# Steps of 512 instead of 256 columns for q, k, v, z and the output projection of a two-layer mixer and mixture-of-experts kernel

## The chip, the cores and the metric

The kernel is one program on one core of a Trainium2 chip. Its time is the device time in microseconds of one execution. The engines are named as in the profile: PE multiplies matrices (PEld is its weight load), DVE and ACT work element by element, POOL is the fourth compute engine, SP issues most of the DMAs. Each engine works through its own queue in order, so an instruction that waits holds up everything behind it on that engine.

## The reference

Two layers over 512 tokens (256 context tokens and 256 latent tokens) of width 1024. The first half of a layer is a mixer of three branches:

```python
h = modulate(x, c)                                    # (512 tokens, 1024)
q, k, v, lru_x, lru_gate, z, xbc, dt, gates = split(h @ w_in)
att = diff_attn(rope(q), rope(k), v)                  # 4 heads, 2 maps each
lru = rglru_bidir(conv(lru_x)) * gelu(lru_gate)       # two linear scans over time
ssd = norm(mamba2_bidir(conv(xbc), dt) * silu(z))     # chunks of 128 tokens
m   = sum(sigmoid(gate_br) * (branch_br @ w_branch[br]) for br in 3)
x   = LN(alpha * x + gate * (m @ w_out))
```

The second half is a mixture of 64 experts (8 per token) and a shared one, with which the change has nothing to do. q, k, v and z are 512 columns each of `w_in`; `w_out` is 1024 by 1024. The second layer needs q, z and the output only for the 256 latent tokens.

## The kernel before

All products that the change touches are made of three matmuls per 128 rows of the sum: activations and weights are split into a high and a low part, and high*high, high*low and low*high are added up in one PSUM bank (`tok`, L566; `w_out`, L1094). The sum has 1024 rows, so a product takes 8 x 3 = 24 matmuls. The activations of a block of 128 tokens are the stationary operand, the weights move through: 256 columns at a time.

The weights come from HBM in chunks of 1 MB (`Main`, L505): 1024 rows of 256 columns. `load` brings a chunk into one of two buffers, `split` makes the high part on ACT and the low part on DVE (two instructions each), `next(i)` splits chunk i+1 and hands out chunk i. `order` says which chunks come when: four of xbc, two of lx, then q, k, v for the first 256 columns and q, k, v for the second, two of lg (the gate of the LRU), two gates g(1,0) and g(1,1), two of z, and the other ten gates. The four chunks of `w_out` follow.

For q and k, each block of 128 tokens goes through one loop step: `tok` puts 24 matmuls into one of the two "mm" banks; `flush(1)` issues the PE transposes of an earlier block's result; three DVE multiplies and a POOL add apply the rotary embedding (blocks 0 and 1) or an ACT copy takes the block out of PSUM (blocks 2 and 3); `side.pump(2.6)` issues a few pieces of side work. v has an ACT copy in place of the rotary embedding. Transposed halves land in the two "tr" banks, from which a DVE copy takes them.

The side work is a set of Python generators (class `Side`, L175): the steps of the SSD branch, of the LRU, of attention and of the modulation for the next layer. `pump` picks the first one whose last step is done by a small clock model, and issues its next step on all engines at once, behind what stands in their queues. `need` issues all that is left of some generators. It is called ahead of lg (all of the LRU), and ahead of g(1,0) (all of the SSD and the LRU).

After the mixer, `w_out` runs over the four (second layer: two) blocks of 128 tokens, a pair of 256-column calls for each 512-column bank, all in the "mm" banks.

Of the kernel before, what the change touches and what calls it, by code (L numbers as in the profile page):

```python
# [13 lines left out]
AF = mybir.ActivationFunctionType  # L14
# [4 lines left out]
P = 128  # L19
# [211 lines left out]
def tile_kernel(ctx: ExitStack, tc: tile.TileContext, A: dict, out: bass.AP):  # L231
# [306 lines left out]
    def feat(hT, w, j, t0, t1, p):  # L538
# [4 lines left out]
            PE.matmul(p[:, t0:t1], w[1][:, k, c], hT(0, k)[:, t0:t1], start=False, stop=k == KD - 1)  # L543
        return p

    def mixer(l, main, order, hT, pre, late):
        last = l == DEPTH - 1
        prm = LP[l]
# [14 lines left out]
        def xt(n):  # L563
            return xA[:, n, :] if n < 4 else xB[:, n - 4, :]

        def tok(w, b, n=256):  # L566
            p = bank("mm")
            c = slice(b * P, (b + 1) * P)
            for k in range(KD):
                PE.matmul(p[:, :n], hT(0, k)[:, c], w[0][:, k, :n], start=k == 0, stop=False)  # L570
                PE.matmul(p[:, :n], hT(0, k)[:, c], w[1][:, k, :n], start=False, stop=False)
                PE.matmul(p[:, :n], hT(1, k)[:, c], w[0][:, k, :n], start=False, stop=k == KD - 1)
            return p
# [281 lines left out]
        def flush(keep=0):  # L855
            while len(pend) > keep:
                dst, r = pend.pop(0)
                pt = bank("tr")
                for h in range(2):
                    PE.transpose(pt[:, h * P:(h + 1) * P], r[:, h * P:(h + 1) * P], ident)  # L860
                V.tensor_copy(dst, pt[:, :256].rearrange("p (h t) -> p h t", h=2))
# [7 lines left out]
                G.tensor_tensor(x_, x_, sg, op=OP.mult)  # L869

        for i, (kind, arg) in enumerate(order):
            w = main.next(i)
            if kind == "lx":
                for j in range(2):
                    n = 2 * arg + j
# [38 lines left out]
                    silu()  # L914
                    g_ssd = side.add(ssd())
            elif kind in "qk":
                if late and kind == "k" and arg == 0:
                    side.add(late)
                dst = (qT if kind == "q" else kT)[:, 2 * arg:2 * arg + 2, :]
                for b in range(nb if kind == "q" else 4):  # L920
                    p = tok(w, b)[:, :256]
                    flush(1)
                    r = tmp()
                    if b < 2:
                        pv = p.rearrange("p (g a f) -> p g a f", g=4, a=2)
                        rv = r[:, :256].rearrange("p (g a f) -> p g a f", g=4, a=2)
                        tv = r[:, 256:].rearrange("p (g a f) -> p g a f", g=4, a=2)
                        V.tensor_mul(rv, pv, rope[:, b, None, None, 0:32].to_broadcast([P, 4, 2, 32]))
                        V.tensor_mul(tv[:, :, 0, :], pv[:, :, 1, :], nsin[:, b, None, :].to_broadcast([P, 4, 32]))
                        V.tensor_mul(tv[:, :, 1, :], pv[:, :, 0, :], rope[:, b, None, 32:64].to_broadcast([P, 4, 32]))  # L930
                        G.tensor_tensor(r[:, :256], r[:, :256], r[:, 256:], op=OP.add)
                    else:
                        S.activation(r[:, :256], p, AF.Copy)
                    pend.append((dst[:, :, b * P:(b + 1) * P], r))
                    side.pump(2.6)
            elif kind == "v":
                for b in range(4):
                    p = tok(w, b)
                    S.activation(vt[:, b, arg * 256:(arg + 1) * 256], p[:, :256], AF.Copy)
                    flush()  # L940
                    side.pump(2.6)
                units += [(2 * arg + h, b) for b in range(nb) for h in range(2)]
                if arg == 1:
                    state["qkv"] = 1
            elif kind == "lg":
                side.need(g_lru)
                if arg == 1 and g_ssd not in side.q:
# [8 lines left out]
                    side.pump(nw)  # L956
            elif kind == "z":
                side.need(g_ssd)
                for b in range(nb):
                    p = tok(w, b)[:, :256]  # L960
                    c = slice(arg * 256, (arg + 1) * 256)
                    z = tmp()
                    S.activation(z[:, :256], p, AF.Sigmoid)
                    V.tensor_mul(z[:, :256], z[:, :256], p)
                    G.tensor_tensor(yd[:, b, c], yd[:, b, c], z[:, :256], op=OP.mult)
                    if arg == 1:
                        LN.setdefault("norm", []).append(side.add(ssd_norm(b)))
                    side.pump(2.6)
            else:
                br, jq = arg  # L970
                ib = 4 * (1, 2, 0).index(br) + jq
# [84 lines left out]
    def sublayer2(l, mg, wo, R):  # L1056
# [36 lines left out]

        def w_out(b, q):  # L1094
            if q % 2 == 0:
                hvs.setdefault(b, []).append(bank("mm"))
            p = hvs[b][-1]
            tk = slice(b * P, (b + 1) * P)
            c = slice(q % 2 * 256, (q % 2 + 1) * 256)
            w = wo[len(order) + q]  # L1100
            for k in range(KD):
                PE.matmul(p[:, c], mg(0, k)[:, tk], w[0][:, k, :], start=k == 0, stop=False)
                PE.matmul(p[:, c], mg(0, k)[:, tk], w[1][:, k, :], start=False, stop=False)
                PE.matmul(p[:, c], mg(1, k)[:, tk], w[0][:, k, :], start=False, stop=k == KD - 1)

        def norm1(b):
            x_ = xr(b)
# [773 lines left out]
    cols += [("w_out", q) for q in range(4)]  # L1881


    mains = [Main(l, cols) for l in range(DEPTH)]
# [178 lines left out]
def _tiles(a, rows, cols):  # L2063

    *lead, r, c = a.shape
    a = a.reshape(*lead, r // (rows * P), rows, P, c // cols, cols)
    n = len(lead)
    a = a.transpose(*range(n), n, n + 3, n + 2, n + 1, n + 4)
    return a.reshape(*lead, r // (rows * P) * (c // cols), P, rows * cols)


def _layouts(inputs):
    import numpy as np
    a = {n: np.asarray(inputs[n]) for n in _INS}
    w = a["w_in"]
    a["w_in"] = np.concatenate([_tiles(w[:, :, :C_DT], KD, 256), _tiles(w[:, :, C_G:], KD, 256)], axis=1)
    a["w_dt"] = _tiles(w[:, :, C_DT:C_G], KD, 16)[:, 0]
    for n in ("w_mod", "w_out"):
        a[n] = _tiles(a[n], KD, 256)
# [31 lines left out]
```

## Time and profile before

| | us |
|---|---|
| median of 3 runs | 2388.75 |
| lowest and highest | 2381.78 and 2395.73 |
| the profiled execution, its own time | 2394.08 |
| its span | 2392.3 |
| PE busy in the span | 2197.0 (92%) |
| mean granted TensorE clock | 0.963 |

In a timeline row the first number is the start in the span, the second the time from the first instruction's start to the last one's end; xN is how many instructions the row holds, and the bracket how long the engine had stood idle before the row and whose result ended that. In a table of windows each engine has its busy time and its count of instructions, followed by the granted TensorE clock (1.00 is 2.4 GHz, 0.50 is 1.2 GHz). The stretches that the change touches: in layer 0, q, k and v from 133.9 to 263.85 us, lg and the forced end of SSD and LRU from 263.85 to 304.25, z from 363.5 to 407, the output projection from 608.3; in layer 1, 1519.2 to 1616.3, 1616.3 to 1640, 1645 to 1670, and from 1788.9.

### The profile page before, as it was taken

Reading aid. Unit: us, or ns where it says so; the run is one execution under the profiler, and the core shown is the slowest. Engines: PE = TensorE matmul, PEld = TensorE weight load, DVE = VectorE, ACT = ScalarE, POOL = GpSimd, SP = SyncE. Lnnn points to the kernel's source line nnn. Section 1 sums busy time; section 2 is a strip of 40 time slices with the busy share of each in tenths; the row PEclk is TensorE's granted clock in tenths of the full one; section 3 lists DMA queues with packets and bytes.
Section 4 is the critical chain, followed back from the end, with each engine's and each line's share of the span. In section 5 each row is a group of like instructions: output and inputs, shape, how many; then the busy total and the mean of one; then the engine's idle time right before and its main releaser. Section 6 shows DMA issues by size and latency. Waiting matters only on the chain. (4 is left out here: it accounts for less than half of the span.)

```text
span 2392.3 us, 37529 instructions
## 1 busy us (share of the span) xinstructions
PE 2197.0 (92%) x14847; PEld 1383.5 (58%) x14847; DVE 1038.9 (43%) x2325; ACT 701.4 (29%) x1270; POOL 450.2 (19%) x388
## 2 busy tenths in 40 slices
PE   7999999999979999999998849998999899999997
PEld 5778767777954334333333228787996444554553
DVE  3756355433653323332222166656665323333333
ACT  3465356423221111111111124655652111111111
POOL 0223111021113223233232144441110000000000
PEclk8999989999979999999999969998999999999999
DMA  7333333453658999999999942113447689999992
GB/s 296 145 139 109 126 125 112 161 186 133 229 224 288 358 375 350 358 354 351 343 354 353 377 147 76 69 70 102 141 169 304 263 360 421 379 420 420 421 420 92
DMA packets 107219, 605.24 MB, mean 253 GB/s; under 512 B 18216, under 2 KB 18560, under 8 KB 42784
## 3 DMA queue, kind: packets, MB, share of 16 engines
q1 hardware_dynamic: 91608, 560.97, 60.6%
q0 software_dynamic: 13952, 41.57, 7.2%
q8 instruction: 118, 1.93, 0.3%
q10 hardware_dynamic: 1480, 0.27, 0.1%
q14 instruction: 61, 0.50, 0.1%
HBM read 576.54 MB, written 31.06 MB: 254 GB/s over the span
## 5 line engine op out<-in xcount | busy, mean ns | idle before, releaser
L149 PE MATMUL mm<-s,t 128*32 128x512 f32 (+3 forms) x4320 | 664.1, 565 | 29.1 <-DMA s<-in_w_up_dram 26.6
L149 PE MATMUL mm<-s,s 128*128 128x256 f32 (+1 forms) x3488 | 561.8, 319 | 13.5 <-DVE tm L149 8.1
L149 PEld LDWEIGHTS mm<-s,s 128*128 128x128 f32 x3488 | 491.1, 194 | 70.3 <-issue 17.9
L149 PEld LDWEIGHTS mm<-s,t 128*32 128x32 f32 (+2 forms) x4320 | 262.8, 127 | 363.4 <-issue 300.3
L149 DVE TENSOR_TENSOR tm<-tm,mm 128x256 f32<-128x256 f32 (+3 forms) x194 | 85.7, 442 | 559.4 <-ACT tm L149 506.8
L149 ACT ACTIVATE tm<-mm 128x256 f32<-128x256 f32 (+3 forms) x155 | 65.1, 421 | 729.3 <-PE mm L149 720.1
L149 DVE TENSOR_TENSOR s<-s,s 128x1024 fp32r<-128x1024 f32 (+4 forms) x170 | 202.3, 1231 | 46.3 <-ACT s L149 43.8
L149 PE MATMUL sd<-s,tm 128*32 128x512 f32 (+2 forms) x1112 | 182.3, 626 | 21.5 <-DMA s<-in_w_down_dram 21.1
L149 POOL DMA_INDIRECT acc<-s,si x77 | 111.1, 1442 | 461.9 <-ACT t L149 226.8
L149 PE MATMUL sd<-s,s 128*128 128x512 f32 (+4 forms) x768 | 183.5, 454 | 12.2 <-ACT t L149 11.2
L149 PEld LDWEIGHTS sd<-s,s 128*128 128x128 f32 (+2 forms) x768 | 112.1, 188 | 68.4 <-issue 33.3
L149 ACT ACTIVATE s<-s 128x1024 fp32r<-128x1024 f32 (+3 forms) x168 | 148.4, 937 | 7.4 <-PE sd L149 6.1
L149 PEld LDWEIGHTS tr<-t,s 128*128 128x128 f32 x1024 | 123.8, 196 | 44.3 <-issue 41.5
L149 PEld LDWEIGHTS sd<-s,tm 128*32 128x32 f32 (+2 forms) x1112 | 54.7, 122 | 142.4 <-issue 114.8
L149 PE MATMUL tr<-t,s 128*128 128x128 f32 (+1 forms) x1024 | 132.6, 284 | 1.4 <-ACT s L149 1.0
L149 POOL TENSOR_TENSOR s<-s,tm 128x512 f32<-128x512 f32 (+1 forms) x52 | 64.0, 1232 | 318.6 <-ACT tm L149 157.3
L149 PE MATMUL mm<-s,tm 128*32 128x512 f32 (+1 forms) x760 | 109.0, 599 | 13.9 <-ACT tm L149 10.2
L149 ACT ACTIVATE t<-tr 128x512 f32<-128x512 f32 (+6 forms) x115 | 62.1, 544 | 184.2 <-PE tr L149 171.6
L149 POOL TENSOR_TENSOR t<-t,mhalf 128x2 f32<-128x2 f32 x1 | 0.7, 702 | 562.9 <-DVE t L149 562.9
L149 PEld LDWEIGHTS tr<-ident,s 128*128 128x128 f32 (+2 forms) x568 | 67.7, 150 | 65.4 <-issue 44.7
L149 PE MATMUL tr<-ident,s 128*128 128x128 f32 (+2 forms) x568 | 83.3, 292 | 24.1 <-DVE s L149 18.4
L149 ACT ACT_TABLE_LOAD x63 | 80.8, 1283 | 39.0 <-PE mm L149 12.9
(255 smaller groups left out, 2161.6 us busy)
## 6 DMA issues: line engine op xcount, KB each, us to landing
s<-in_w_up_dram SPq DMA_DIRECT2D x256, 1024.0 KB
s<-in_w_down_dram SPq DMA_DIRECT2D x128, 1024.0 KB
s<-in_w_in_dram SPq DMA_DIRECT2D x56, 1024.0 KB
s<-in_w_mod_dram SPq DMA_DIRECT2D x48, 1024.0 KB
t<-in_w_branch_dram SPq DMA_DIRECT2D x32, 256.0 KB
s<-in_w_out_dram SPq DMA_DIRECT2D x8, 1024.0 KB
acc<-t SPq DMA_DIRECT2D x4, 1280.0 KB
s<-in_ws_up_dram SPq DMA_DIRECT2D x4, 1024.0 KB
```

Source lines behind the costliest of these rows:

```text
L149: r = f(*a, **k)
```

## The change

The weights of q, k, v, z and `w_out` are laid out in other chunks of 1 MB: 512 rows of 512 columns ("half 0" and "half 1" of the rows). A product of 1024 rows and 512 columns needs two chunks; its 24 matmuls are 512 wide, and it fills a whole bank. The number of chunks, of buffers and of bytes stays.

`tok` takes the blocks of tokens in pairs: 12 matmuls of half 0 for the first block and 12 for the second, then 12 of half 1 for each. Only then are the two results handed on, one after the other, with the same steps as before for each of their 256-column halves. So four steps of flush, rotary embedding and pump follow one another, where before one step followed each 24 matmuls. v and z have one 512-wide step per block. The order of chunks is q, q, k, k, v, v. In `w_out` the banks alternate between "mm" and "sd".

```diff
-        def tok(w, b, n=256):
-            p = bank("mm")
-            c = slice(b * P, (b + 1) * P)
-            for k in range(KD):
-                PE.matmul(p[:, :n], hT(0, k)[:, c], w[0][:, k, :n], start=k == 0, stop=False)
...
+        def tok(i, blocks):
+            main.split(i + 1)
+            hl = [wide(main.hl.pop(i + q)) for q in range(2)]
+            for b0 in range(0, blocks, 2):
+                bs = range(b0, min(b0 + 2, blocks))
+                ps_ = {b: bank("mm") for b in bs}
+                for q in range(2):
+                    if q and b0 + 2 >= blocks:
+                        main.split(i + 2)
+                    for b in bs:
+                        p, c, w = ps_[b], slice(b * P, (b + 1) * P), hl[q]
+                        for k in range(4):
+                            kk = 4 * q + k
+                            PE.matmul(p, hT(0, kk)[:, c], w[0][:, k, :], start=kk == 0, stop=False)
+                            PE.matmul(p, hT(0, kk)[:, c], w[1][:, k, :], start=False, stop=False)
+                            PE.matmul(p, hT(1, kk)[:, c], w[0][:, k, :], start=False, stop=kk == KD - 1)
+                for b in bs:
+                    yield b, ps_[b]
...
-                for b in range(nb if kind == "q" else 4):
-                    p = tok(w, b)[:, :256]
-                    flush(1)
...
+                for b, pp in tok(i, nb if kind == "q" else 4):
+                    for hh in range(2):
+                        p = pp[:, hh * 256:(hh + 1) * 256]
+                        flush(1)
...
-                    S.activation(vt[:, b, arg * 256:(arg + 1) * 256], p[:, :256], AF.Copy)
+                for b, p in tok(i, 4):
+                    S.activation(vt[:, b, :], p, AF.Copy)
                     flush()
-                    side.pump(2.6)
-                units += [(2 * arg + h, b) for b in range(nb) for h in range(2)]
+                    side.pump(5.2)
+                units += [(h, b) for b in range(nb) for h in range(4)]
...
-                hvs.setdefault(b, []).append(bank("mm"))
+                hvs.setdefault(b, []).append(bank("mm" if b % 2 == 0 else "sd"))
...
-            for k in range(KD):
-                PE.matmul(p[:, c], mg(0, k)[:, tk], w[0][:, k, :], start=k == 0, stop=False)
...
+            for k in range(4):
+                kk = 4 * (q % 2) + k
+                PE.matmul(p, mg(0, kk)[:, tk], w[0][:, k, :], start=kk == 0, stop=False)
...
-    for hh in range(2):
-        order += [("q", hh), ("k", hh), ("v", hh)]
+    order += [(n, i) for n in "qkv" for i in range(2)]
```

Three places show how instructions move. The first is DVE's queue in layer 0 around the first results of q. Here `tm` are the rotary results (`mm_74` and `mm_75` the two banks of PSUM they come from), the products `t_852` and `t_853` belong to the SSD, the SCALAR_TENSOR_TENSOR rows on `s_121` and `s_123` with the add into `s_131` are the scans of the LRU, and the COPY takes a transposed result out of a "tr" bank. Before:

```order
L149 TENSOR_TENSOR tm_73<-mm_74,rope 128x256
...
L149 TENSOR_TENSOR tm_71<-mm_75,rope 128x256
L149 TENSOR_TENSOR tm_71<-mm_75,nsin 128x4x32
L149 TENSOR_TENSOR tm_71<-mm_75,rope 128x4x32
L149 TENSOR_TENSOR mrows<-mrows,tr_80 128x256
L149 TENSOR_TENSOR t_852<-t_852,t_905 128x512
L149 TENSOR_TENSOR t_853<-t_853,t_905 128x512
L149 SCALAR_TENSOR_TENSOR s_121<-s_121 128x256 x2
L149 SCALAR_TENSOR_TENSOR s_123<-s_121,s_123 128x512
L149 TENSOR_TENSOR s_131<-s_121,s_123 128x512
L149 COPY s_369<-tr_81 128x2x128
```

And after the change:

```order
L149 TENSOR_TENSOR tm_73<-mm_74,rope 128x256
...
L149 TENSOR_TENSOR mrows<-mrows,tr_80 128x256
L149 TENSOR_TENSOR t_852<-t_852,t_905 128x512
L149 TENSOR_TENSOR t_853<-t_853,t_905 128x512
L149 SCALAR_TENSOR_TENSOR s_121<-s_121 128x256 x2
L149 SCALAR_TENSOR_TENSOR s_123<-s_121,s_123 128x512
L149 TENSOR_TENSOR s_131<-s_121,s_123 128x512
L149 TENSOR_TENSOR tm_71<-mm_74,rope 128x256
L149 TENSOR_TENSOR tm_71<-mm_74,nsin 128x4x32
L149 TENSOR_TENSOR tm_71<-mm_74,rope 128x4x32
L149 COPY s_369<-tr_81 128x2x128
```

The second rotary result (`tm_71`) stood ahead of the side work and now stands behind it.

The second place is PE's queue at the same spot. `sd_76` and `sd_77` are products of the SSD, and the rows with `ident,tm` the transposes of the rotary results. Before:

```order
L149 MATMUL mm_75<-s_312,s_178 128x256
L149 MATMUL tr_80<-s_125,sT 32x256 x8
L149 MATMUL sd_76<-t_852,mask_95 128x512
L149 MATMUL sd_77<-t_853,mask_96 128x512
L149 MATMUL mm_74<-s_312,s_175 128x256
...
L149 MATMUL mm_74<-s_313,s_176 128x256
L149 MATMUL mm_74<-s_312,s_178 128x256
L149 MATMUL tr_81<-ident,tm_73 128x128 x2
```

And after the change:

```order
L149 MATMUL mm_75<-s_375,s_178 128x512
L149 MATMUL tr_80<-s_125,sT 32x256 x8
L149 MATMUL sd_76<-t_852,mask_95 128x512
L149 MATMUL sd_77<-t_853,mask_96 128x512
L149 MATMUL tr_81<-ident,tm_73 128x128 x2
L149 MATMUL tr_80<-ident,tm_71 128x128 x2
L149 MATMUL tr_81<-s_125,sT 32x256 x8
```

A block of 24 matmuls stood between the side work and the first transposes; now both transposes follow the side work directly.

The third place is POOL's queue at the first results of q in layer 1. Rows with `tm` alone are the adds of the rotary embedding, the others belong to the LRU (`s_153`, `s_155`) and the SSD. Before:

```order
L149 TENSOR_TENSOR t_374<-t_374,t_4411 128x512
L149 TENSOR_TENSOR t_926<-t_926,t_4412 128x512
L149 TENSOR_TENSOR tm_71<-tm_71 128x256
L149 TENSOR_TENSOR tm_72<-tm_72 128x256
L149 TENSOR_TENSOR s_153<-s_153 128x512
L149 TENSOR_TENSOR s_155<-s_155 128x512
```

And after the change:

```order
L149 TENSOR_TENSOR t_374<-t_374,t_4011 128x512
L149 TENSOR_TENSOR t_926<-t_926,t_4012 128x512
L149 TENSOR_TENSOR tm_73<-tm_73 128x256
L149 TENSOR_TENSOR s_153<-s_153 128x512
L149 TENSOR_TENSOR s_155<-s_155 128x512
L149 TENSOR_TENSOR t_4012<-t_117,dec 128x512
L149 TENSOR_TENSOR t_851<-mask_94,av 128x512
L149 TENSOR_TENSOR t_853<-mask_94,av 128x512
L149 TENSOR_TENSOR tm_71<-tm_71 128x256
L149 TENSOR_TENSOR tm_72<-tm_72 128x256
```

The second rotary add followed the first; now five instructions of side work stand between them.

## Rows read from the trace of the kernel before

**Rows 1.** The page's first part: busy time of each engine

```profile
PE 2197.0 (92%) x14847; PEld 1383.5 (58%) x14847; DVE 1038.9 (43%) x2325; ACT 701.4 (29%) x1270; POOL 450.2 (19%) x388
```

**Rows 2.** Windows: layer 0 q, k, v; layer 0 z; layer 1 q, k, v

```profile
133.90:263.85 129.95, 127.90 (x1003) 107.04 (x1001) 80.04 (x152) 67.66 (x101) 42.35 (x36) 1.00 0.34 123
...
363.50:407.00 43.50, 37.96 (x293) 32.61 (x292) 24.06 (x58) 28.57 (x65) 8.94 (x14) 0.96 0.34 121
...
1519.20:1616.30 97.10, 93.87 (x683) 80.83 (x683) 62.06 (x93) 62.04 (x89) 43.76 (x34) 1.00 0.19 66
```

**Rows 3.** Timeline of PE: long runs of 512 and of 256 columns

```profile
590.33 11.04 PE L149 MATMUL mm<-s,s 128*128 128x512 f32 x48
...
1606.09 8.87 PE L149 MATMUL mm<-s,s 128*128 128x256 f32 x72
```

**Rows 4.** Timeline of PE: waits in the stretches of the change

```profile
300.54 4.28 PE L149 MATMUL sd<-t,s 128*128 128x256 f32 x8 [3.37 <-POOL t L149]
...
396.63 4.37 PE L149 MATMUL mm<-s,s 128*128 128x256 f32 x24 [3.45 <-DVE tm L149]
...
608.31 2.77 PE L149 MATMUL mm<-s,s 128*128 128x256 f32 x21 [0.92 <-DVE tm L149]
612.41 0.50 PE L149 MATMUL mm<-s,s 128*128 128x256 f32 x2 [1.33 <-ACT s L149]
...
1623.63 8.89 PE L149 MATMUL mm<-s,s 128*128 128x256 f32 x70 [0.95 <-DVE s L149]
...
1640.23 4.13 PE L149 MATMUL sd<-s,s 64*128 64x512 f32 x8 [5.79 <-ACT t L149]
...
1654.96 5.49 PE L149 MATMUL mm<-s,s 128*128 128x256 f32 x24 [2.83 <-DVE s L149]
```

**Rows 5.** Timeline of DVE: scans, rotary multiplies, products of the SSD

```profile
145.30 1.47 DVE L149 TENSOR_TENSOR_SCAN s<-s 128x256 f32<-128x256 f32 x2
...
147.92 0.69 DVE L149 TENSOR_TENSOR s<-s,s 128x512 f32<-128x512 f32 x1
...
166.33 0.41 DVE L149 TENSOR_TENSOR tm<-mm,rope 128x256 f32<-128x256 f32 x1
...
167.05 0.41 DVE L149 COPY s<-tr 128x256 f32<-128x256 f32 x1
...
176.28 1.28 DVE L149 TENSOR_TENSOR t<-t,t 128x512 f32<-128x512 f32 x2
```

**Rows 6.** Timeline of POOL: rotary add, side work of both layers

```profile
167.30 0.73 POOL L149 TENSOR_TENSOR tm<-tm 128x256 f32<-128x256 f32 x1 [7.13 <-DVE tm L149]
167.99 2.54 POOL L149 TENSOR_TENSOR s<-s 128x512 f32<-128x512 f32 x2
...
1529.11 3.99 POOL L149 TENSOR_TENSOR s<-s 128x512 f32<-128x512 f32 x2
...
1535.04 1.04 POOL L149 TENSOR_TENSOR t<-mask,av 128x512 f32<-128x512 f32 x1
```

**Rows 7.** Timeline of ACT: one gate step of the LRU in layer 1

```profile
1601.20 0.69 ACT L149 ACTIVATE s<-sd,pc 128x512 f32<-128x512 f32 x1 [0.17 <-PE sd L149]
1601.90 1.28 ACT L149 ACT_TABLE_LOAD   x1
1603.20 2.85 ACT L149 ACTIVATE s<-s,nl 128x512 f32<-128x512 f32 x4
...
1610.93 1.15 ACT L149 ACTIVATE s<-s 128x512 f32<-128x512 f32 x2
```

**Rows 8.** Timelines of DVE and POOL: the chunk-to-chunk carry of the SSD

```profile
297.64 1.72 DVE L149 TENSOR_TENSOR t<-t,dec 128x512 f32<-128x512 f32 x2
...
298.84 3.85 POOL L149 TENSOR_TENSOR t<-t,t 128x512 f32<-128x512 f32 x2 [0.63 <-DVE t L149]
```

**Rows 9.** Windows: PE after the waits at 396.63 and 1654.96

```profile
396.60:401.00 4.40, 4.37 (x25) 4.37 (x26) 3.95 (x10) 0.28 (x1) 1.46 (x2) 0.66 0.96 343
...
1654.90:1660.30 5.40, 5.34 (x25) 5.34 (x26) 3.21 (x5) 0.27 (x1) 0.00 (x0) 0.50 0.34 86
```

More of the change, by code (lines that the diff above doesn't have):

```diff
@@ L544, in feat, with wide @@
         return p
+    def wide(hl):
+        return [fold(w.rearrange("p k c -> p (k c)"), (4, 512)) for w in hl]
     def mixer(l, main, order, hT, pre, late):
@@ L871, in mixer @@
         for i, (kind, arg) in enumerate(order):
-            w = main.next(i)
+            if kind in "qkvz":
+                if arg:
+                    continue
+            else:
+                w = main.next(i)
             if kind == "lx":
@@ L916, in mixer @@
             elif kind in "qk":
-                if late and kind == "k" and arg == 0:
+                if late and kind == "k":
                     side.add(late)
-                dst = (qT if kind == "q" else kT)[:, 2 * arg:2 * arg + 2, :]
-                for b in range(nb if kind == "q" else 4):
-                    p = tok(w, b)[:, :256]
-                    flush(1)
[L923 to L934, printed above, removed]
-                    side.pump(2.6)
@@ new lines, in mixer @@
+                dst = qT if kind == "q" else kT
+                for b, pp in tok(i, nb if kind == "q" else 4):
+                    for hh in range(2):
+                        p = pp[:, hh * 256:(hh + 1) * 256]
+                        flush(1)
+                        r = tmp()
+                        if b < 2:
+                            pv = p.rearrange("p (g a f) -> p g a f", g=4, a=2)
+                            rv = r[:, :256].rearrange("p (g a f) -> p g a f", g=4, a=2)
+                            tv = r[:, 256:].rearrange("p (g a f) -> p g a f", g=4, a=2)
+                            V.tensor_mul(rv, pv, rope[:, b, None, None, 0:32].to_broadcast([P, 4, 2, 32]))
+                            V.tensor_mul(tv[:, :, 0, :], pv[:, :, 1, :], nsin[:, b, None, :].to_broadcast([P, 4, 32]))
+                            V.tensor_mul(tv[:, :, 1, :], pv[:, :, 0, :], rope[:, b, None, 32:64].to_broadcast([P, 4, 32]))
+                            G.tensor_tensor(r[:, :256], r[:, :256], r[:, 256:], op=OP.add)
+                        else:
+                            S.activation(r[:, :256], p, AF.Copy)
+                        pend.append((dst[:, 2 * hh:2 * hh + 2, b * P:(b + 1) * P], r))
+                        side.pump(2.6)
@@ L945, in mixer @@
+                units += [(h, b) for b in range(nb) for h in range(4)]
+                state["qkv"] = 1
             elif kind == "lg":
@@ L958, in mixer @@
                 side.need(g_ssd)
-                for b in range(nb):
-                    p = tok(w, b)[:, :256]
-                    c = slice(arg * 256, (arg + 1) * 256)
+                for b, p in tok(i, nb):
                     z = tmp()
[L963 to L968, printed above, removed]
+                    S.activation(z, p, AF.Sigmoid)
+                    V.tensor_mul(z, z, p)
+                    G.tensor_tensor(yd[:, b, :], yd[:, b, :], z, op=OP.mult)
+                    LN.setdefault("norm", []).append(side.add(ssd_norm(b)))
+                    side.pump(5.2)
             else:
@@ L1880, in tile_kernel @@
     cols = [("w_in", 16 + a[0] * 4 + a[1] if k == "g" else CO[k][0] // 256 + a) for k, a in order]
-    cols += [("w_out", q) for q in range(4)]
+    cols += [("w_out", q % 2 * 2 + q // 2) for q in range(4)]
     mains = [Main(l, cols) for l in range(DEPTH)]
@@ L2075, in _layouts @@
     w = a["w_in"]
-    a["w_in"] = np.concatenate([_tiles(w[:, :, :C_DT], KD, 256), _tiles(w[:, :, C_G:], KD, 256)], axis=1)
+    a["w_in"] = np.concatenate([_tiles(w[:, :, c:c + 512], 4 if c in (C_Q, C_K, C_V, C_Z) else KD,
+                                       512 if c in (C_Q, C_K, C_V, C_Z) else 256) for c in range(0, C_DT, 512)]
+                               + [_tiles(w[:, :, C_G:], KD, 256)], axis=1)
     a["w_dt"] = _tiles(w[:, :, C_DT:C_G], KD, 16)[:, 0]
-    for n in ("w_mod", "w_out"):
-        a[n] = _tiles(a[n], KD, 256)
+    a["w_mod"] = _tiles(a["w_mod"], KD, 256)
+    a["w_out"] = _tiles(a["w_out"], 4, 512)
     a["w_branch"] = _tiles(a["w_branch"], 4, P)
```

15 lines of the change are left out of this document (3 added, 12 removed).

## The prediction, made before the changed kernel ran

> **What bounds the kernel now.** The first view is the page's busy time: PE works 2197.0 of 2392.3 us, the next engine, DVE, 1038.9 [rows 1]. So whatever PE does less is gained, and whatever it waits more is lost, unless another limit steps in. The second view is the windows of the stretches that the change touches, because an average over the span hides them. In layer 0's q, k and v PE is busy 127.90 of 129.95 us, in layer 1's 93.87 of 97.10, both at a granted clock of 1.00 [rows 2]: 2.05 and 3.23 us of idle time, almost nothing, although DVE, ACT and POOL do a lot of side work in them (80, 68 and 42 us in layer 0). In layer 0's z it is 37.96 of 43.50: 5.54 us idle at 0.96. The third view is the waits of PE by timeline, which names the larger ones [rows 4]; the fourth is what DVE, POOL and ACT do in the same places [rows 5 to 8].
>
> **Part 1, the matmuls: 15 us less.** 72 matmuls of 256 columns take 8.87 us, 123 ns each; 48 of 512 take 11.04, 230 ns each [rows 3]. Two narrow ones are 246 ns, so a wide one saves 16 ns, and a product of 24 wide ones 0.39 us. How many products: layer 0 has q, k, v and z over 4 blocks each, 16, and the output projection with 4 blocks of two banks, 8, together 24; layer 1 has 2 + 4 + 4 + 2 = 12, and 2 x 2 = 4, together 16. 40 x 0.39 is 15.6 us. Each of the two rows holds one end effect, so I take 15. The ends: 0, if runs of only 12 lose at their edges what the width saves, and 17.
>
> The Trainium skill ("TensorE: Matmul & The Clock Gate", section "Back-to-back issue gap") gives a warm isolated gap of N/2.4 + 2.5 ns. By it two of 256 columns cost 218.3 ns and one of 512 215.8, so an estimate from that page is 2.5 ns for a pair and 2.4 us for all 960 pairs. The trace disagrees with this by its 16 ns a pair.
>
> **Part 2, what a pair of blocks does to the queues: 23 us more.** Before, the three steps of a block's result (rotary multiplies, POOL add, transposes on PE) are a block apart: PE issues 24 matmuls, some 3 us, before it comes to the transposes. After, PE's transposes stand right behind the side work that followed the first result, and on DVE and POOL the second result stands behind the same side work (the order of the change). PE cannot pass a transpose that waits; the next pair's matmuls, some 11 us of work, are queued behind it, and the weight split and DMAs behind those.
>
> - Layer 0, first pair of q. PE runs the SSD's two mask products and the transposes of the first result. The second result waits on DVE for two products, 1.28, that need ACT's exponentials of these very mask products, then the scans with their add, 145.30 to 148.61, 3.31, then its own three multiplies, 166.33 to 167.05, 0.72 [rows 5], and POOL's add, 0.73 [rows 6]. Sum 6.0, while the exponentials before it are covered by PE's own transposes. I take 6.0.
> - The other pairs there: q's second and k's first have only products of 1.28 and a rotary step of 0.72 in front of the DVE copy that frees the "tr" bank: 2.0 and 2.1. k's second has the scans, 3.31, and an 0.69 add: 4.0. Half 1 of the first pair comes before its split is done: 0.8, a choice by the DVE queue ahead of it. Layer 0: 14.9.
> - Layer 1, q's pair: POOL has two LRU products, 2.54 alone and 3.99 beside DVE [rows 6], three products of 1.04, and the add, 0.73, so 6.4 to 7.8 between the two rotary adds. They can start up to 2.8 us before the pair ends, when the first block's bank is full (12 matmuls of 0.23). That gives 3.6 to 7.8; I take 5.5. k's two pairs: the exponentials of the masks stand behind four sigmoids (2.8) and a table load (1.28), 4.1 [rows 7], so 4.2; and again the scans, 3.31 with copy and multiplies behind, 3.9. Layer 1: 13.6.
>
> Together 28.5. The idle time of before in these two stretches, 2.05 + 3.23 [rows 2], goes: 23.2 net. The ends are -5 (the second result is ready in time at every pair, and the old waits vanish) and 33 (each wait a third larger, as POOL's 3.99 against 2.54 would have it).
>
> The skill's "Perfetto Trace Analysis", section "Matmuls", wants independent groups to rotate through PSUM banks, so that emptying one overlaps the next group's matmuls, and it calls larger matmuls more efficient. Its first half speaks against handing on both banks together, its second for the change. By the second half alone part 2 would be zero. A trace row with PE waiting for a bank to be emptied is the 3.45 us on a rotary or gate temporary [rows 4], which goes with the first half.
>
> **Part 3, side work that is forced later: 7 us more.** v pumps four times instead of eight, so more of the SSD and LRU is left when `need` issues it in one go. In layer 0 the carry then shows: before, PE waited 3.37 for POOL's 3.85 behind DVE's 1.72 [rows 4, 8]; after, the last masks' exponentials and products come on top, 3. In layer 1 the last LRU gate step is forced just ahead of lg, and ACT has four sigmoids 2.76, four exponentials 2.85, the square roots 1.15 and three table loads 3.84 in front of the Gelu that frees the first bank, 10.6 [rows 7]; lg's own 48 matmuls hide 5.9 [rows 3]; 4.7 is left, against 0.95 now [rows 4]: 3.8 more. Its carry, hidden before, costs POOL's 3.85 behind the last two of DVE's products, 1.28 [rows 5, 8]: 5.1, taken as 5. Against this the 5.79 us wait that follows, for an ACT result of attention [rows 4], is mostly absorbed, since attention then has had more time: 4.5 less. 3 + 3.8 + 5 - 4.5 = 7.3. Ends: -6 and 12 (nothing of 5.79 absorbed).
>
> **Part 4, z and the output projection: 7 us less.** z in layer 0 has two 512-wide steps a pair in place of eight small ones; of its 5.54 us of waits [rows 2] I leave 1. In the output projection the first call needs only half of the sum that the mixer leaves, so its two first waits, 0.92 and 1.33 [rows 4], go. 4.5 + 2.2 = 6.7. Ends: 0 and 8.
>
> **Part 5, the clock: 8 us more.** Where PE has waited long, the next matmuls run at a lower granted clock: 24 products of 256 columns took 4.37 us after the wait of 3.45 and 5.49 after 2.83, at 0.66 and 0.50 [rows 4, 9], against 2.96 (24 of the 72) at full clock. That is 1.4 and 2.5. In layer 1's q, k, v with its short waits the clock stayed at 1.00 [rows 2]. Of the new waits seven are above 3.4 us (6.0, 4.0, 5.5, 4.2, 3.9, 4.7, 5); two old ones go (3.45, 5.79). Five more at 1.4 to 2.5 is 7 to 12; I take 8.
>
> **Sum.** -15 + 23.2 + 7.3 - 6.7 + 8 = +16.8. The profiled execution's own time is 2394.08, so it would be 2411; it lies 5.3 above the median of the runs shown, 2388.75, so the median after would be 2405.6, and I say 2406. The mixture of experts has the same instructions in the same order and moves along.
>
> **The rivals.**
> - The queues keep up, and the gain stays. The first block's bank is full 2.8 us before the pair ends; if DVE, POOL and ACT use that head start, part 2 is at most 6, part 3 no more than -2, part 5 nothing: -15 + 6 - 2 - 6.7 = -18, 2371; with 12 in part 2, 2377. For it: DVE is busy 62% of layer 0's stretch, so there is room on the average. Against it: on DVE the side products wait for mask products that PE runs only after the pair, so the head start is of no use there. It decides when the waits of part 2 are under some 12 us.
> - Waits and gain cancel. Part 2 at half, 11, part 3 at 4, part 5 at 3: -15 + 11 + 4 - 6.7 + 3 = -4, 2385. The side work that was put off may then be found waiting with its inputs ready.
> - Waits and clock feed each other: part 2 at 33, part 3 at 12 and part 5 at 14: -15 + 33 + 12 - 6.7 + 14 = +37, 2426. For it: POOL's 3.99 against 2.54 beside a busy DVE [rows 6]; against it, some waits stand together and share one fall of the clock.
> - The wide matmuls save nothing, since their runs are only 12 long: part 1 is 0, and the sum +32, 2421. Against it, the runs of 48 and 72 [rows 3] consist of the same kind of matmul, and nothing in them changes at the twelfth. The skill's gap, above, is the nearest rule to this rival.
>
> **How the numbers follow.** Chances: forecast 0.44, gain stays 0.14, cancel 0.24, feed each other 0.14, nothing saved 0.04. Slower by over 0.5% (above 2400.7; 12 us is about what a measurement of this kernel tells from no change) is forecast, third and fourth rival: 0.62. Within is 0.24, faster 0.14. The forecast's own range is 2397 to 2417. The range that holds 8 in 10 leaves out the better half of the first rival and the worse of the third: 2377 to 2428.
>
> **What would show it.** Long runs of 512 columns at 227 to 230 ns in q, k, v show part 1. Part 2 shows as waits of PE at the transposes `tr<-ident,tm`, one at each pair's end, 6 us for the first in layer 0, released by POOL's add or DVE's copy, and a busy share of PE in the first stretch near 0.89 (14.9 us idle of some 130) instead of 0.98. Part 3 shows as a wait of PE in lg of layer 1, released by ACT. Part 4 shows as a z without the wait of 3.45. Part 5 shows as windows at 0.5 to 0.75 behind the waits, and a mean clock below 0.963. The prediction is wrong if the transposes find their results ready, or if the wide matmuls hide so much more side work that PE's queue never comes to them too early.

## The result: 57 us slower, more than three times the loss that was forecast

The median of six runs is 2449.54 us (2442.49 to 2453.2), that of the kernel before 2388.86. The medians differ by 61 us; the ratio on record is 1.0238, with a 95% interval from 1.0217 to 1.0258, which makes 57. The profiled execution is among the shortest of the six, 2442.88, and that of the kernel before lies above its median, so the two traces below differ by 48.6 us only. What the medians differ by beyond that, these two traces cannot show.

The page after, first part, answers to [rows 1]:

```profile
PE 2204.3 (90%) x13887; PEld 1342.5 (55%) x13887; DVE 1026.5 (42%) x2319; ACT 706.1 (29%) x1261; POOL 442.3 (18%) x382
```

PE has 960 matmuls less and is busy 7.3 us longer, and it idles 236.6 us in place of 195.3. Both are against the change. Windows tell where they come from. The columns are as in [rows 2]: stretch, its length, busy time of PE, PEld, DVE, ACT, POOL, then the granted clock. After, layer 0: q, k and v; lg and the forced end of the side work; from there to the output projection; the projection. Layer 1: q, k and v; lg and the forced end.

```profile
131.95:276.20 144.25, 128.95 (x652) 92.55 (x651) 68.17 (x117) 64.91 (x90) 38.97 (x33) 0.91 0.30 104
276.20:332.56 56.36, 49.77 (x266) 38.76 (x263) 25.89 (x58) 17.45 (x26) 15.00 (x12) 0.85 0.37 136
332.56:633.56 301.00, 289.17 (x1582) 217.66 (x1581) 145.03 (x291) 132.01 (x265) 41.03 (x40) 0.99 0.40 143
633.56:702.90 69.34, 58.82 (x295) 48.99 (x295) 48.54 (x119) 21.06 (x44) 14.22 (x12) 0.94 0.69 262
...
1536.90:1640.25 103.35, 89.98 (x392) 64.94 (x391) 47.58 (x82) 51.82 (x70) 28.26 (x26) 0.90 0.17 62
1640.25:1680.80 40.55, 24.82 (x150) 22.35 (x149) 18.76 (x22) 20.34 (x26) 14.45 (x13) 0.80 0.28 97
```

The stretches before that go with the second to fourth and with the last of these (the first and third of [rows 2] go with the other two):

```profile
263.85:304.25 40.40, 36.90 (x202) 27.81 (x201) 17.23 (x22) 14.43 (x18) 11.48 (x8) 0.94 0.37 131
304.25:608.31 304.06, 292.84 (x1678) 224.83 (x1676) 145.27 (x296) 129.78 (x267) 42.10 (x44) 0.98 0.42 146
608.31:682.10 73.79, 63.07 (x487) 61.70 (x487) 48.92 (x121) 21.09 (x44) 14.20 (x12) 0.90 0.66 247
...
1616.34:1629.70 13.36, 12.41 (x100) 12.01 (x99) 10.93 (x10) 5.27 (x7) 6.45 (x6) 1.00 0.25 86
```

Read as differences of length, after less before: layer 0's q, k, v +14.3, its lg +16.0, then -3.1 for the stretch with z and -4.5 for the projection; layer 1's q, k, v +6.2, its lg +27.2. So the loss is in q, k, v and in lg behind them. These two have to be read together, 30.3 us in layer 0 and 33.4 in layer 1, because side work moved from one to the other: lg now holds 64 and 50 matmuls more (266 for 202, 150 for 100). The two stretches where no transposes of the results follow the products at once, z's and the projection, got shorter. The granted clock fell from 1.00 to 0.91 and 0.90 in q, k, v, in layer 0's lg from 0.94 to 0.85, and in layer 1's from 1.00 to 0.80.

The waits of PE after, in the manner of [rows 4]; the bracket has the idle time and what ended it:

```profile
153.52 0.69 PE L149 MATMUL tr<-ident,tm 128*128 128x128 f32 x2 [5.96 <-POOL tm L149]
208.69 0.41 PE L149 MATMUL tr<-ident,tm 128*128 128x128 f32 x2 [1.38 <-DVE s L149]
237.66 0.66 PE L149 MATMUL tr<-ident,tm 128*128 128x128 f32 x2 [5.25 <-DVE s L149]
...
329.35 3.78 PE L149 MATMUL sd<-t,s 128*128 128x256 f32 x8 [4.57 <-POOL t L149]
...
441.71 1.38 PE L149 MATMUL tr<-s,sT 128*32 128x256 f32 x16 [3.63 <-DMA s<-in_w_mod_dram]
...
1554.98 0.69 PE L149 MATMUL tr<-ident,tm 128*128 128x128 f32 x2 [5.74 <-POOL tm L149]
1578.73 0.50 PE L149 MATMUL tr<-ident,tm 128*128 128x128 f32 x2 [3.69 <-POOL tm L149]
1601.38 0.66 PE L149 MATMUL tr<-ident,tm 128*128 128x128 f32 x2 [3.73 <-DVE s L149]
1655.13 5.49 PE L149 MATMUL mm<-s,s 128*128 128x256 f32 x24 [8.86 <-ACT tm L149]
1677.58 3.78 PE L149 MATMUL sd<-t,s 128*128 128x256 f32 x8 [6.87 <-POOL t L149]
```

These are the longer ones. All the waits on `tr<-ident,tm` stand at pair ends, and the first is 5.96 us where 6.0 was forecast. DVE's timeline in front of it shows the chain link by link, as [rows 5] had priced it: two products, the scans, and only then the second rotary step:

```profile
145.50 0.42 DVE L149 TENSOR_TENSOR mrows<-mrows,tr 128x256 f32<-128x256 f32 x1 [2.80 <-PE tr L149]
147.15 0.69 DVE L149 TENSOR_TENSOR t<-t,t 128x512 f32<-128x512 f32 x1 [1.23 <-ACT t L149]
148.01 0.69 DVE L149 TENSOR_TENSOR t<-t,t 128x512 f32<-128x512 f32 x1 [0.17 <-ACT t L149]
148.62 1.47 DVE L149 TENSOR_TENSOR_SCAN s<-s 128x256 f32<-128x256 f32 x2
...
151.85 0.42 DVE L149 TENSOR_TENSOR tm<-mm,rope 128x256 f32<-128x256 f32 x1
```

The first result's bank was full some 2.8 us before the pair's end, and DVE took its first half out at once. Then it stood idle, 2.80 us for transposes and 1.23 us for exponentials of mask products, and PE runs both, the transposes and the products, only after the pair.

What a wait does to the clock, in windows of the first wait after: the wait, and the three stretches behind it:

```profile
147.50:153.50 6.00, 0.06 (x1) 0.00 (x0) 5.76 (x13) 0.48 (x1) 0.72 (x1) 0.89 0.36 152
153.50:158.00 4.50, 4.48 (x28) 2.88 (x28) 1.76 (x10) 1.67 (x2) 1.45 (x2) 0.50 0.14 27
158.00:163.00 5.00, 5.00 (x25) 5.00 (x25) 0.00 (x0) 0.00 (x0) 0.00 (x0) 0.50 0.44 185
163.00:168.00 5.00, 5.00 (x21) 2.06 (x20) 0.69 (x1) 1.64 (x3) 0.35 (x1) 0.71 0.00 0
...
210.00:220.00 10.00, 10.00 (x38) 8.81 (x38) 2.62 (x9) 0.10 (x1) 4.03 (x5) 0.51 0.14 60
```

PE is busy the whole time from 153.5 on, at 0.50, 0.50 and 0.71. By these clocks the 14.5 us hold the work of some 8.3 at full clock, an estimate. The last row stands behind the wait of only 1.38 us at 208.69.

### The profile page after: what moved, and what is told of

Its sections match the earlier page's. It is cut to its first block, busy times and chain, and to the rows that moved or that the text cites. A ratio compares the mean times of both kernels' runs of the same rounds, so it can differ in the third digit from the quotient of the medians.

```text
span 2440.9 us, 35570 instructions
## 1 busy us (share of the span) xinstructions
PE 2204.3 (90%) x13887; PEld 1342.5 (55%) x13887; DVE 1026.5 (42%) x2319; ACT 706.1 (29%) x1261; POOL 442.3 (18%) x382
## 5 line engine op out<-in xcount | busy, mean ns | idle before, releaser
L149 PE MATMUL mm<-s,s 128*128 128x512 f32 (+1 forms) x2384 | 507.4, 371 | 14.4 <-ACT tm L149 8.9
L149 PEld LDWEIGHTS mm<-s,s 128*128 128x128 f32 x2384 | 408.6, 193 | 99.6 <-issue 14.5
L149 DVE TENSOR_TENSOR tm<-tm,mm 128x256 f32<-128x256 f32 (+2 forms) x188 | 84.9, 452 | 555.2 <-ACT tm L149 504.3
L149 ACT ACTIVATE tm<-mm 128x256 f32<-128x256 f32 (+2 forms) x149 | 63.8, 431 | 691.8 <-PE mm L149 682.8
L149 PE MATMUL sd<-s,s 128*128 128x512 f32 (+4 forms) x912 | 220.4, 451 | 6.5 <-ACT t L149 5.4
L149 DVE TENSOR_TENSOR s<-s,s 128x1024 fp32r<-128x1024 f32 (+5 forms) x170 | 199.3, 1210 | 55.9 <-ACT s L149 51.6
L149 PEld LDWEIGHTS sd<-s,s 128*128 128x128 f32 (+2 forms) x912 | 138.7, 189 | 70.9 <-issue 37.1
L149 ACT ACT_TABLE_LOAD x68 | 87.2, 1283 | 34.7 <-DVE s L149 14.8
```

What stands on the lines that cost most here:

```text
L149: r = f(*a, **k)
```

## The experiments

**Which part of the change.** Two kernels, each with one half of the change. The first keeps `w_out` at 512 columns (chunks, calls and banks of the change) and leaves q, k, v, z as before; the second is its mirror image.

```diff
+            w = wide(wo[len(order) + q])
+            for k in range(4):
+                kk = 4 * (q % 2) + k
+                PE.matmul(p, mg(0, kk)[:, tk], w[0][:, k, :], start=kk == 0, stop=False)
...
```

> The kernel before with the output projection alone in steps of 512 columns (its chunks, its bank order, its calls); q, k, v, z as before. In the two traces the stretch of the projection went from 73.8 to 69.3 us in layer 0 and from 29.5 to 28.1 in layer 1. Theory (the loss comes from q and k alone, the width itself gains): 6 us faster than before, 2383. Rival (wide matmuls in half-row chunks cost as much as they save, and what the projection gained came from elsewhere): 2389, no difference.

Measured: 2381.28 us, ratio 0.9957 (0.9937 to 0.9977): faster by 0.4%, as expected.

> The changed kernel with the output projection put back to 256 columns; q, k, v and z wide. Theory (all of the loss is in q, k, v and what follows from them): 61 + 6 = 67 us slower than before, 2455. Rival (part of the loss is in the projection's other banks and later start): 2445 or less.

Measured: 2453.47, ratio 1.0256 (1.0221 to 1.0291). So the whole loss is there without the wide projection: it is in q, k, v, z and what follows. That the projection gains in the changed kernel too, is not shown by the times, since this interval and that of the changed kernel (1.0217 to 1.0258) overlap.

**Is it the bunch or the width?** The kernel before, with its narrow matmuls and its chunks, but in q and k the matmuls of all blocks first and their results after:

```diff
-                for b in range(nb if kind == "q" else 4):
-                    p = tok(w, b)[:, :256]
+                nq, ps_ = nb if kind == "q" else 4, {}
+                for b in range(nq):
+                    if b % 2 == 0:
+                        pw = bank("mm")
+                    ps_[b] = tok(w, b, 256, pw, (b % 2) * 256)
+                for b in range(nq):
+                    p = ps_[b]
```

> The kernel before (256 columns, its chunks and their order), but q and k put the matmuls of all their blocks first and then hand on the results one after the other, two blocks in one bank. Theory (it is the bunch of results, not the width): PE waits of 4 to 6 us behind the bunches of q and k in both layers, released by POOL's rotary adds and DVE's copies, 20 us of waits and 15 of clock: 2425. Rival (width or half-row chunks are what costs): 2389, as before.

Measured: 2433.44, ratio 1.0162 (1.0125 to 1.0198). Waits in layer 0 behind the first bunch of q, the first of k and the second of q, from PE's timeline of this kernel:

```profile
153.44 0.69 PE L149 MATMUL tr<-ident,tm 128*128 128x128 f32 x2 [5.95 <-POOL tm L149]
...
192.63 0.69 PE L149 MATMUL tr<-ident,tm 128*128 128x128 f32 x2 [4.36 <-POOL tm L149]
...
242.23 0.66 PE L149 MATMUL tr<-ident,tm 128*128 128x128 f32 x2 [4.64 <-DVE s L149]
```

Not one matmul is wider than before and not one chunk cut otherwise, and the first wait is 5.95 us. So the bunch alone makes these waits. Windows of this kernel show how far that reaches: q, k, v in layer 0 and in layer 1, and lg in layer 1.

```profile
132.29:292.77 160.48, 139.10 (x999) 112.68 (x997) 76.02 (x152) 66.64 (x99) 40.35 (x36) 0.89 0.29 100
...
1554.35:1660.51 106.16, 100.05 (x684) 86.32 (x684) 63.24 (x93) 63.40 (x90) 44.44 (x34) 0.94 0.18 60
1660.51:1672.21 11.70, 11.70 (x98) 11.67 (x97) 11.46 (x10) 5.27 (x7) 7.92 (x6) 1.00 0.25 91
```

In layer 0 they take 30.5 us more than before, as much as the change costs in q, k, v and lg together. In layer 1 they take only 9.1 more, with one wait of 3.71 where waits of 4 to 6 were expected, and lg has no idle time at all. So the 33.4 us that the change loses in layer 1 are for the most part not explained by bunches of q and k.

**Is it the order in the queues?** The changed kernel, pairs as they are, but the rotary steps (512 wide) of both blocks issued ahead of the side work:

```diff
+                for b, p in tok(i, nb if kind == "q" else 4):
+                    if b % 2 == 0:
+                        flush()
+                        r, sc_, r1 = tmp(), tmp(), tmp()
...
+                    if b % 2:
+                        for g in got:
+                            flush(1)
+                            pend.append(g)
+                            side.pump(2.6)
```

> The changed kernel, pairs of blocks as they are, but the rotary steps (or copies) of both blocks are issued ahead of the side work, 512 wide, and the four transposes and pumps follow. Theory (the second result waits because it stands behind scans and products in DVE's and POOL's queues): the waits of 5.96 (layer 0) and 5.74 (layer 1) at the first pair of q go to under 2, the one of 3.69 as well; those on the copy out of the bank (5.25, 3.73) may stay since the copies still stand behind scans; 13 us of waits and some 8 of clock: 2428. Rival (the side work itself is what PE waits for, whatever the order): same waits with other names, 2445 to 2450.

Measured: 2415.29, ratio 1.0097 (1.0063 to 1.0132), 34 us of the loss back where 21 were expected. The windows of q, k, v and of lg, in layer 0 and then in layer 1:

```profile
130.85:250.65 119.80, 112.48 (x641) 81.72 (x639) 60.29 (x97) 54.85 (x73) 32.82 (x26) 1.00 0.36 125
250.65:306.79 56.14, 50.08 (x278) 37.75 (x275) 34.64 (x65) 26.65 (x38) 19.99 (x16) 0.95 0.38 136
...
1519.22:1604.66 85.44, 81.72 (x388) 59.70 (x387) 50.47 (x69) 44.41 (x59) 28.80 (x20) 1.00 0.21 74
1604.66:1655.19 50.53, 28.79 (x154) 24.69 (x153) 21.05 (x23) 28.73 (x37) 16.93 (x15) 0.74 0.23 78
```

With this order (and rotary steps half as many and twice as wide, which the run does not separate from it) q, k, v lose their long waits, the longest that is left is 2.62 us, and the clock is back at 1.00 in both layers. They take 119.8 and 85.4 us, less than before the change, part of their side work being done in lg as in the changed kernel. What is left is lg of layer 1, where the LRU's last steps are forced: its wait for ACT grew from 8.86 to 15.68.

**One block at a time.** Both halves of the rows for a block, then its two results:

```diff
-            for b0 in range(0, blocks, 2):
...
+            for b in range(blocks):
+                p, c = bank("mm"), slice(b * P, (b + 1) * P)
                 for q in range(2):
```

> The changed kernel, but one block of tokens at a time: 24 matmuls of 512 columns (both halves of the rows) and then this block's two results, in place of two blocks and then four results. Theory (results of a pair handed on together put the transposes behind side work with no matmuls between): a block's second result now has 24 matmuls, 5.5 us, ahead of its transposes, so the waits of 5.96, 5.25, 5.74, 3.69 and 3.73 us at pair ends fall under 2 each, the clock stays up in these stretches, some 19 us of waits and 12 of clock come back: 2418; the waits in lg (8.86, 6.87, 4.57) stay. Rival (what costs is the side work that v pumps half as often and that is forced later): pair-end waits matter little, 2440 to 2450.

Measured: 2416.6, ratio 1.0102 (1.0065 to 1.0138): the expected size, though not in every part. Four of the five waits at pair ends fell under 2 us; the one of 5.74 at layer 1's first q is still 4.97. In lg of layer 1 the two waits that were expected to stay are gone, with 0.99 left, but one of 8.62 for ACT stands right behind lg. And the trace has a cost that was not expected: a step's first block now needs half 1 right after half 0, and its split is not done. One of six such places, in layer 1 (about 14 us for all six):

```profile
1596.30 0.50 PE L149 MATMUL mm<-s,s 128*128 128x512 f32 x1 [2.33 <-ACT s L149]
1597.56 4.15 PE L149 MATMUL mm<-s,s 128*128 128x512 f32 x11 [0.76 <-DVE s L149]
```

The change's pairs hide most of this split behind the second block's half 0; 0.72 and 0.21 us are left there, at the first pair of q. So a chunk of half the rows has its own price when it is used at once.

**The clock.** The changed kernel with 20 extra matmuls ahead of the transposes that wait longest, in the first pair of q of each layer. They write the "tr" bank that the transposes then overwrite.

```diff
+                        if kind == "q" and b == 1 and hh == 1:
+                            warm = banks["tr"][turn["tr"] % 2]
+                            for n in range(20):
+                                PE.matmul(warm, hT(0, n % KD)[:, :P], hT(0, n % KD), start=True, stop=True)
                         flush(1)
```

> The changed kernel with 20 extra matmuls of 512 columns (4.5 us, results overwritten) in each layer's first pair of q, right ahead of the transposes that wait 5.96 and 5.74 us there; nothing else differs. Theory (PE's clock is granted lower after it has stood still, and the busy time behind such a wait grows): the waits shrink to some 1.5 us, the granted clock behind the one in layer 0 stays near 1.00 instead of 0.50 to 0.71 over 153 to 168 us, and 5 us there and 1 to 2 in layer 1 come back: 2442. Rival (the lower clock has to do with the wide matmuls or the side work, not with the wait): clock as in the changed kernel, 2449 or a little more.

Measured: 2441.11, ratio 1.0200 (1.0172 to 1.0229): 8.4 us less than the changed kernel by the medians, though 9.6 us of work were added; the two ratios' intervals overlap, so the time alone does not show it and the trace has to. The windows around the first wait:

```profile
147.50:153.50 6.00, 6.00 (x26) 4.22 (x24) 4.60 (x7) 1.20 (x2) 0.00 (x0) 1.00 0.50 175
153.50:158.00 4.50, 3.10 (x33) 2.22 (x33) 3.26 (x15) 1.45 (x2) 2.18 (x3) 1.00 0.06 15
158.00:163.00 5.00, 5.00 (x36) 3.38 (x37) 0.69 (x1) 1.31 (x3) 0.00 (x0) 1.00 0.50 200
```

The wait is 1.40 us long now, and the clock stays at 1.00. From the late transposes to the next wait the trace has 25.2 us (155.03 to 180.22), against 31.0 in the changed kernel (153.52 to 184.52); both end with the same wait of 1.70. The same stretch in layer 1 went from 23.8 to 22.1. So the lower clock behind one wait of 6 us had cost 5.8 us here and 1.7 there. Little of that is kept to the end of v: q, k, v are shorter by 3.2 us in layer 0 (141.09 against 144.25) and not at all in layer 1 (103.46 against 103.35), since the clock now stays low for longer behind later waits. The clearest case is k's second pair in layer 0, whose wait is the same in both kernels, 5.25 and 5.24 us. The 12.2 us behind it, first in the changed kernel, then in this one:

```profile
237.60:249.80 12.20, 12.14 (x70) 7.45 (x71) 9.17 (x14) 7.48 (x10) 8.36 (x6) 0.86 0.27 88
...
231.70:243.90 12.20, 12.18 (x50) 6.39 (x52) 6.60 (x10) 4.99 (x7) 7.86 (x6) 0.50 0.24 88
```

PE is busy in both, at 0.86 in the one and at 0.50 in the other.

**More pumps in v.** Two pumps a block, as many as before the change.

```diff
-                    side.pump(5.2)
+                    side.pump(2.6)
+                    side.pump(2.6)
```

> The changed kernel with two pumps of side work for each block of v instead of one, so as many as before the change. My prediction's part 3 (v pumps half as often, so side work is left over and forced at lg): the waits in layer 1's lg, 8.86 and 6.87 us, go under 3 each and with them some 5 us of lower clock, 2433. Rival (pumps find no side step ready, because everything that a bunch of four results issues is still in the queues): the order of instructions hardly changes, 2449.

A call of `pump` issues up to four steps, and its number only credits one slow generator, so two calls can issue twice as many steps as one. Measured: 2448.38, ratio 1.0223 (1.0186 to 1.0260), the rival's time. The wait in layer 1's lg is 8.87, as it was, and the side work stands in the same order as in the changed kernel, but for one step of the modulation and one copy in layer 0. So a second pump at the same place finds nothing ready. That is less than the eight pumps of before, which had matmuls between them.

**Everything spread.** Wide matmuls, pairs and the order of chunks stay, but after each 12 matmuls one result is transposed and one pump made, and a block's rotary step is issued as soon as its matmuls are.

```diff
-                for b in bs:
-                    yield b, ps_[b]
+                        yield b, p if q else None
...
+                    if p is None:
+                        flush(2 - b % 2)
                         side.pump(2.6)
+                        continue
...
+                    flush(2 + b % 2)
+                    side.pump(2.6)
```

> The changed kernel's chunks, wide matmuls, pairs and order of chunks, but the work around them is spread: after each 12 matmuls one transposed result and one pump of side work (in q, k, v and z), and a block's rotary step is issued as soon as its own matmuls are, 512 wide, so as many steps per microsecond of matmuls as before the change. Theory (the bunching costs all of it, the width gains): waits of PE in q, k, v as before the change, 2 to 4 us a layer, clock there at 0.98 or more, the matmuls 12 to 15 us less and the output projection its 6: 2370 to 2378, faster than before. Rival (half-row chunks, which need two splits before a product can end, cost of themselves): 2395 or more.

Measured: 2398.59, ratio 1.0023 (1.0003 to 1.0042). 51 us of the 61 come back, but the kernel isn't faster than before: a miss. The time is the rival's, but its reason is not in the trace, where PE waits for no split of a half-row chunk in q, k and v. Layer 1 is as good as before: its q, k, v and lg take 112.8 us (1533.46 to 1646.26), against 110.5 before and 143.9 in the changed kernel, and lg has no wait. The largest waits of PE that are left, from its timeline:

```profile
325.44 4.45 PE L149 MATMUL sd<-s,s 64*128 64x512 f32 x8 [5.15 <-ACT t L149]
...
419.08 1.22 PE L149 MATMUL mm<-s,s 128*128 128x512 f32 x2 [4.99 <-DVE tm L149]
...
1550.41 0.69 PE L149 MATMUL tr<-ident,tm 128*128 128x128 f32 x2 [5.28 <-POOL tm L149]
```

In layer 0's q, k, v no wait is above 2.7 us now; the large ones stand behind it, in attention's products and in z. From g(1,0) to the projection layer 0 takes 315.7 us (306.15 to 621.83) against 304.1. That attention's units are all appended after the last chunk of v, where half of them came with the first chunk before, is not enough to explain it: the changed kernel appends them in the same way and takes 301.0 us there. The cause stays open. And one wait at layer 1's first pair survived: it ends with POOL's first rotary add, which starts at 1549.10, right behind 8 us of side work on POOL.

**A version that beats both.** z has no transposes right behind it (PE comes to them only two chunks of gates later), so it should take the width too:

```diff
+            if kind == "z":
+                if arg:
+                    continue
+            else:
+                w = main.next(i)
...
+                for b, p in tokw(i, nb):
```

> The kernel before with z and the output projection in steps of 512 columns, as in the change; q, k and v stay at 256 columns with a result after each block. Theory (the width gains wherever no bunch of transposes hangs on it; z has none, its results go to ACT, DVE and POOL only): the output projection's 8 to 10 us as in the run with the projection alone, and for z 12 x 0.4 us of matmuls less some wait, 3 to 5 us more: 2377, the fastest of all. Rival (z's results in pairs cost the side work behind them what the width saves): 2381 or more, no better than the projection alone.

Measured: 2380.35, ratio 0.9965 (0.9948 to 0.9982). That is faster than the kernel before, and not to be told from the projection alone (0.9957, 0.9937 to 0.9977). In its trace layer 0's z has waits of 1.65 and 0.46 in place of 3.45, 1.37 and 0.73, so what part 4 of the prediction says of z's waits is seen there, but it is too small to show in the time of the kernel.

## Why the prediction was right in direction and wrong in size

The kernel was forecast 17 us slower and is 57 to 61 slower, outside the range. The mechanism, waits of PE at the transposes and a lower clock behind them, was right; three terms of the sum were mis-sized, all in the change's favour: the clock (part 5), the forced side work (part 3) and what z and the projection would save (part 4). All numbers here are from the two traces, over the stretches from layer 0's q to the projection's end in each layer: PE idles 39 us more there, against 24 forecast (parts 2 to 4), and is busy 13.6 more, where parts 1 and 5 together made 7 less.

- **Part 1, the matmuls: right.** A pair's 48 wide matmuls at full clock took 11.18 us (246.59 in the trace after); runs of 48 narrow ones took 6.00 each (639.85 in the trace before), so 0.4 us a product was gained, 16 us over 40. That is 17 ns for two narrow matmuls. The estimate from the gap that the Trainium skill gives ("TensorE: Matmul & The Clock Gate", section "Back-to-back issue gap"), 2.5 ns, is not what this case shows.
- **Part 2, the pair ends: right.** Idle time of q, k, v rose by 13.3 and 10.1 us, 23.4 against 23.2. The places and the releasers are those named; single waits were up to 1.3 us off (5.25 for 4.0).
- **Part 3, the forced side work: mis-sized.** It was 7.3 in the sum and came to 14.1. Layer 0's lg has 3.1 us more idle time (3 forecast), with the carry's wait at 4.57 after 3.37 [rows 4], but layer 1's 14.8, against 8.8. The wait for ACT was priced from the start of lg; in the trace ACT first stands idle 2.92 us for DVE, which ends the split of a chunk and then a scan of the LRU step before:

```profile
1643.07 1.28 ACT L149 ACT_TABLE_LOAD   x1 [2.92 <-DVE s L149]
1644.36 2.42 ACT L149 ACTIVATE s<-sd,pc 128x512 f32<-128x512 f32 x4
...
1654.69 0.66 ACT L149 ACTIVATE tm<-mm 128x256 f32<-128x256 f32 x2
```

  The chain from there to the Gelu is 11.6 us and was priced nearly right (10.6, with three table loads where it has four); its start was not. The carry, taken as 5, waits 6.87. Of the 5.79 us behind it, 4.5 were to be absorbed; 3.8 were. Why the side work comes late was put down to v's four pumps. Doubling them in place changed nothing. In the three runs where each result of v has matmuls in front of it and a pump behind it (one block at a time, everything spread, narrow with bunches in q and k alone) lg of layer 1 idles at most 0.99 us, and the first of these has four pumps in v as well. In all runs with v's results in pairs the long waits are there. That points to the pairs in v. No run changes v alone, so it isn't shown.
- **Part 4, z and projection: missed.** -6.7 was forecast, and the two stretches idle 0.4 us more. z's waits went, but a wait for a modulation chunk came in the same stretch, 3.63 us on a DMA, so the stretch with it idles 0.6 us more and not 4.5 less. Of the projection's two first waits, the one of 0.92 stayed as it was:

```profile
633.56 5.96 PE L149 MATMUL mm<-s,s 128*128 128x512 f32 x25 [0.92 <-DVE tm L149]
```

  The one of 1.33 became 0.35 and the later ones grew, 3.94 to 4.31 for instance, so the projection idles 0.2 us less and not 2.2.
- **Part 5, the clock: the term that failed most.** 8 us were put in, 1.4 to 2.5 for each of five more waits. With 13.6 us of busy time more in spite of 16 us of matmuls less, the lower clock cost about 29 us, an estimate; a second one, PE's busy time weighted with the granted clock of the same stretches, gives 25 (43 us lost after, 18 before). The two rows that gave the price hold for their two waits [rows 9]. What was missed is how often the clock falls and how long PE then works at the lower level. The granted clock falls to 0.50 fifteen times in these stretches, where it fell seven times before. Behind the first wait it stayed low for some 12 us, and once, around 210 to 220 us, 0.51 followed a wait of only 1.38. The run that fills one such wait shows 5.8 us for it.

The forecast's third rival, waits and clock feeding each other, had the clock at 14 and the sum at +37. Its clock term comes nearest and is still half of what the traces show; the waits of part 2 that it wanted, 33, did not come (23.4).

## What to carry to other kernels

When a product is made larger, look first at what is issued between products: results that were handed on one at a time come in a bunch, and in in-order queues they then stand behind side work that used to stand behind them. Price a new wait of the matrix engine by its length and by the slower stretch behind it, read to the end of that stretch. Wide steps paid where no transpose of the result is the next thing in the matrix engine's queue (the output projection here, 0.4%), and not where it is.

## What the runs showed of the hardware that was not expected

A wait of 6 us was followed by 12 us in which PE, busy without a gap, was granted 0.50 to 0.71 of full speed, that is mostly the level of 1.2 GHz. A wait of nearly the same length in layer 1, 5.74 us, was followed by a shorter stretch:

```profile
1555.00:1557.00 2.00, 2.00 (x7) 1.73 (x7) 1.30 (x5) 0.00 (x0) 0.60 (x1) 0.50 0.00 0
1557.00:1562.00 5.00, 5.00 (x20) 3.99 (x20) 4.93 (x6) 3.77 (x4) 0.95 (x1) 0.85 0.02 3
```

Filling these waits with 4.8 us of useless matmuls kept the clock at 1.00 right behind them, and by that the lower clock had cost 5.8 us behind the one and 1.7 behind the other, a factor of three. One and the same wait, 5.25 and 5.24 us at k's second pair, was followed by 12.2 us at 0.86 in the changed kernel and at 0.50 in the one with the first wait filled. So in these traces the length of a wait alone does not tell what the clock takes behind it.
